# Regrouping a batched attention-times-value kernel: four heads as two half units, out stored in 8 KiB runs

## The chip, the cores and the metric

One core of one Trainium2 chip. The metric is the device time of one execution in microseconds (us), as the median of several runs. The program runs on one core. The profile's span, from the first to the last instruction, is some 1.7 to 1.8 us shorter than the timed run.

## The reference

```python
batch, n_heads, seq, head_dim = 8, 12, 1024, 64
# attn_weights: (8, 12, 1024, 1024) float32, v: (8, 12, 1024, 64) float32
out = np.einsum('bhqs,bhsd->bhqd', attn_weights, v).astype(np.float32)
```

There are 96 heads. The attention weights are 402.7 MB, v and out 25.2 MB each.

## The kernel before

Two heads at a time ("a pair", 48 of them) are loaded as 128 rows of 16 row groups, and cast from fp32 to bf16 on the way. TensorE transposes the groups (two bf16 as one fp32 word), VectorE and ScalarE copy them out to `at`, then v is multiplied with them, and the product is copied to `ot`, transposed back, copied to `osb` and stored.

```python
HELD = 9                       # stores of the last nine pairs before the last are issued after the last load
pieces_of = {                  # the last two loads come in pieces of row groups
    NP - 2: [(0, GH), (GH, GH)],
    NP - 1: [(0, 4), (4, 4), (8, 4), (12, 2), (14, 1), (15, 1)],
}

def multiply(i):
    for h in range(2):                         # head
        for half in range(2):                  # half of the row groups = half of the out partitions
            n = 0
            for kw in range(KW):
                for par in range(2):
                    last = pe.matmul(
                        out=po[h][ds(half * D, D)],            # 64 of the 128 partitions
                        lhsT=vbf[i][:, 2 * kw + par, h],       # 64 columns of v
                        rhs=at[:, ds(half * GH, GH), kw, ds(h * HP, HP), par],   # 512 columns
                        start=(n == 0), stop=(n == SB - 1),
                    )
                    n += 1
        last.then_inc(s_m[h])
# ... (cut)
def pe_direct(p):      # the last pair: each row group is multiplied as it arrives, straight into out order
    # ... (cut)
    last = pe.matmul(out=x[:, g - g0], lhsT=at[:, g, kw, :, par],
                     rhs=vbf[i][:, 2 * kw + par].rearrange("p h d -> p (h d)"), ...)
# ... (cut)
def store(p, by_sync=False):
    eng = nc.sync if by_sync else pool
    eng.wait_ge(s_out, p + 1)
    eng.dma_start(out=out_p[p].rearrange("p g d -> p (g d)"),      # 128 runs of 4 KiB
                  in_=osb[p % NO].rearrange("p g d -> p (g d)"),
                  **({} if by_sync else {"single_packet": True}))
```

## Time and profile before

| | before |
|---|---|
| time | 1056.73 us, 3 runs (1056.70 to 1056.76) |
| span of the profiled run | 1055.0 us |
| busy share of TensorE / VectorE / ScalarE | 75% / 37% / 38% |
| GpSimd's DMA queue | 99.5% of 16 engines' span |
| mean granted TensorE clock (share of full speed that the chip allowed) | 0.874 |

The prediction below shows the lines of the page, the chain and the windows. A busy share is an average over the whole run. What a change is worth is read from two stages: the beats of two pairs, which the loads set, and the tail after the last load, where the stores drain and the last pair is computed. Two more lines are needed. The first is of the timeline of before (start, length, engine, line, operation, tiles, count): the multiply of the pair before the last. The second is SyncE, which issues held stores as soon as the piece with groups 12 and 13 of the last load has landed.

```profile
1025.65 4.81 PE L173 MATMUL bank<-at,vbf 128*64 128x512 bf16 x32
...
1038.14 2.84 SPq L389 DMA_DIRECT2D out_dram<-osb  x6
```

So 32 matmuls of 512 columns take 4.81 us, 150 ns each, and at 1038.1 all of the last load had landed but its groups 14 and 15.

### The profile page before, as it was taken

The numbers are of one execution on the slowest core, as the hardware profiler recorded it, in microseconds if no ns is written. First come the engines' busy times: TensorE is split into PE (matmuls) and PEld (weight loads), VectorE is DVE, ScalarE is ACT, GpSimd is POOL, SyncE is SP. The second block draws the span as 40 slices with busy tenths as digits, with TensorE's granted clock in tenths as the row PEclk, the third lists the DMA queues.
The fourth block names the chain that finished last, engine by engine and source line by source line (L and its number), as shares of the span: only waits on it lengthen the run. The fifth ranks groups of instructions, "written<-read, shape, count | busy, mean of one in ns | idle before, by whom it ended". The sixth has DMA issues, their size and how long they took to land.

```text
span 1055.0 us, 12504 instructions
## 1 busy us (share of the span) xinstructions
PE 791.8 (75%) x5472; PEld 631.6 (60%) x5472; DVE 390.7 (37%) x585; ACT 397.6 (38%) x483; POOL 65.8 (6%) x127
## 2 busy tenths in 40 slices
PE   0897687866878678776787767877678767797797
PEld 0775476645765567555675556655566556675676
DVE  0443344333433334333343333533334333343353
ACT  0353334333434334333344333433334333353353
POOL 1010000100001000000000000000000000000020
PEclk9898878988889879898788988988879898798899
DMA  9999999999999999999999999999999999999998
GB/s 219 219 217 219 238 222 236 219 224 236 236 220 236 219 238 223 234 221 227 232 235 220 227 228 239 220 231 225 236 224 235 220 222 237 216 219 211 218 215 276
DMA packets 18590, 239.76 MB, mean 227 GB/s; under 512 B 2064, under 2 KB 2448, under 8 KB 11920
## 3 DMA queue, kind: packets, MB, share of 16 engines
q0 software_dynamic: 16992, 234.89, 99.5%
q1 hardware_dynamic: 1584, 4.72, 1.2%
q8 instruction: 4, 0.07, 0.0%
q14 instruction: 10, 0.08, 0.0%
HBM read 427.82 MB, written 25.17 MB: 429 GB/s over the span
## 4 chain that ended last, share of the span: by engine, by line
DMA 69%; PE 27%; issue 1%; POOL 1%; ACT 0%; POOLq 0%; DVE 0%; SPq 0%
DMA abf<-in_attn_weights_dram 69%; PE bank L130 23%; PE bank L145 2%; POOL vr L382 1%; PE bank L173 1%; PE bank L224 1%; ACT at L312 0%; PE bank L157 0%; ACT osb L339 0%; ACT vbf L287 0%; POOL abf L376 0%; POOLq L423 0%; DVE osb L299 0%; POOLq L476 0%; SPq L84 0%
## 5 line engine op out<-in xcount | busy, mean ns | idle before, releaser
L130 PE MATMUL bank<-ident,abf 128*128 128x128 f32 x3072 | 466.3, 324 | 256.6 <-DMA abf<-in_attn_weights_dram 256.6
L130 PEld LDWEIGHTS bank<-ident,abf 128*128 128x128 f32 x3072 | 456.4, 215 | 280.0 <-DMA abf<-in_attn_weights_dram 279.1
L312 DVE COPY at<-bank 128x1024 bf16<-128x1024 bf16 x480 | 320.6, 689 | 483.3 <-PE bank L130 481.1
L312 ACT COPY at<-bank 128x1024 bf16<-128x1024 bf16 x288 | 289.1, 1012 | 430.3 <-PE bank L130 430.3
L173 PE MATMUL bank<-at,vbf 128*64 128x512 bf16 x1504 | 226.1, 391 | 0.0
L173 PEld LDWEIGHTS bank<-at,vbf 128*64 128x64 bf16 x1504 | 111.2, 108 | 99.3 <-DVE vbf L287 7.6
L349 ACT COPY ot<-bank 128x512 f32<-128x512 f32 x47 | 27.5, 585 | 192.0 <-PE bank L173 192.0
L349 DVE COPY ot<-bank 128x512 f32<-128x512 f32 x47 | 32.5, 692 | 151.0 <-PE bank L173 151.0
L376 POOL DMA_DIRECT2D abf<-in_attn_weights_dram x54 | 28.9, 537 | 405.6 <-PE bank L130 403.0
L157 PEld LDWEIGHTS bank<-ident,ot 128*128 128x128 f32 x384 | 41.0, 140 | 20.3 <-issue 20.3
L157 PE MATMUL bank<-ident,ot 128*128 128x128 f32 x384 | 52.4, 280 | 0.0
L339 ACT COPY osb<-bank 128x512 f32<-128x512 f32 x94 | 50.5, 589 | 0.4
L145 PE MATMUL bank<-vr,spread 32*128 32x512 bf16 x384 | 50.2, 377 | 0.0
L382 POOL DMA_DIRECT2D vr<-in_v_dram x23 | 12.1, 528 | 496.4 <-PE bank L145 496.4
L287 DVE CAST vbf<-bank 128x512 bf16<-128x512 f32 x48 | 33.2, 692 | 13.6 <-PE bank L145 13.6
L287 ACT CAST vbf<-bank 128x512 bf16<-128x512 f32 x48 | 28.1, 585 | 23.3 <-PE bank L145 23.2
L145 PEld LDWEIGHTS bank<-vr,spread 32*128 32x128 bf16 x384 | 16.0, 92 | 16.4
L389 POOL DMA_DIRECT2D out_dram<-osb x41 | 22.0, 538 | 48.4 <-ACT osb L339 48.3
L224 PE MATMUL bank<-vbf,at 128*128 128x128 bf16 x128 | 8.6, 219 | 1.0 <-ACT osb L339 0.8
L224 PEld LDWEIGHTS bank<-vbf,at 128*128 128x128 bf16 x128 | 7.5, 98 | 1.7 <-ACT osb L339 1.0
L299 DVE COPY osb<-bank 64x256 f32<-64x256 f32 (+1 forms) x5 | 1.8, 361 | 6.4 <-PE bank L224 6.4
L299 ACT COPY osb<-bank 64x256 f32<-64x256 f32 (+1 forms) x5 | 1.6, 325 | 5.3 <-PE bank L224 5.3
(11 smaller groups left out, 7.1 us busy)
## 6 DMA issues: line engine op xcount, KB each, us to landing
abf<-in_attn_weights_dram POOLq DMA_DIRECT2D x46, 4096.0 KB, 32.2
out_dram<-osb POOLq DMA_DIRECT2D x41, 512.0 KB, 32.1
vr<-in_v_dram POOLq DMA_DIRECT2D x23, 512.0 KB, 12.6
abf<-in_attn_weights_dram POOLq DMA_DIRECT2D x2, 2048.0 KB, 26.6
abf<-in_attn_weights_dram POOLq DMA_DIRECT2D x3, 1024.0 KB, 19.2
out_dram<-osb SPq DMA_DIRECT2D x6, 512.0 KB, 8.3
v<-in_v_dram SPq DMA_DIRECT2D x1, 1024.0 KB, 5.2
abf<-in_attn_weights_dram POOLq DMA_DIRECT2D x1, 512.0 KB, 25.5
```

The source lines that it names most:

```text
L130: last = pe.matmul(out=pt[g % 4][:, k], lhsT=words[:, k], rhs=ident, is_transpose=True, start=(k == 0), stop=(k == KW - 1),)
L145: last = pe.matmul(out=po[h], lhsT=spread[rows, b], rhs=vr[rows, b], start=(b == 0), stop=(b == VB - 1),)
L157: last = pe.matmul(out=px[n][:, ds(j * P, P)], lhsT=ot[:, 4 * n + j].rearrange("p h q -> p (h q)"), rhs=ident, is_transpose=True, start=(j ...
L173: last = pe.matmul(out=po[h][ds(half * D, D)], lhsT=vbf[i][:, 2 * kw + par, h], rhs=at[:, ds(half * GH, GH), kw, ds(h * HP, HP), par], sta ...
L224: last = pe.matmul(out=x[:, g - g0], lhsT=at[:, g, kw, :, par], rhs=vbf[i][:, 2 * kw + par].rearrange("p h d -> p (h d)"), start=(n == 0), ...
L287: copy(out=vbf[i][:, :, h], in_=po[h].rearrange("p (k d) -> p k d", k=SB)).then_inc(s_vbf[h])
L312: ins = copy(out=at[:, g].rearrange("c k j two -> c (k j two)"), in_=bank[g % 4].bitcast(bf16),)
L339: last = nc.scalar.copy(out=halves[:, :, ds(4 * n, 4)].rearrange("p half j d -> p j half d"), in_=px[n].rearrange("p (j half d) -> p j hal ...
L349: copy(out=ot[:, :, h], in_=po[h].rearrange("p (j q) -> p j q", j=GH)).then_inc(s_ot[h])
L376: pool.dma_start(out=abf[p % 2][:, ds(g0, gn)].rearrange("p g s -> p (g s)"), in_=attn_p[p][:, ds(g0 * S, gn * S)],).then_inc(s_abf[p % 2] ...
L382: pool.dma_start(out=vr.rearrange("p b x -> p (b x)"), in_=v_g[iv]).then_inc(s_v, 16)
L389: eng.dma_start(out=out_p[p].rearrange("p g d -> p (g d)"), in_=osb[p % NO].rearrange("p g d -> p (g d)"), **({} if by_sync else {"single_ ...
```

## The change

The intent is fewer and longer runs of out. A unit is now one half of the rows of four heads; after two such units the out of four heads stands in 8 KiB runs, and is stored by one transfer. v of four heads is spread once, in the first unit. The last four heads are kept as two two-head units, and the last of them is no longer multiplied group by group. Units are numbered 0 to 47: 45 is the last four-head one, 46 and 47 are the two-head ones, and 47's load comes in four pieces. The core of the diff, with cuts:

```diff
-    HELD = 9
+    HELD = 4
     pieces_of = {
-        NP - 2: [(0, GH), (GH, GH)],
-        NP - 1: [(0, 4), (4, 4), (8, 4), (12, 2), (14, 1), (15, 1)],
+        NU - 2: [(0, GH), (GH, GH)],
+        NU - 1: [(0, 4), (4, 4), (8, 4), (12, 4)],
     }
+    attn_q = attn_weights.rearrange("b (hq four) (p r) s -> (b hq) (four p) (r s)", four=VH, p=VP)
+    out_q = out.rearrange("b (hq four) (p r) d -> (b hq) (four p) (r d)", four=VH, p=VP)
 # ... (cut)
+        def pe_unit(i, n, loaded, it):          # in the loop: 256 columns for each matmul
 # ... (cut)
+            for hp in range(2):
+                for h in range(2):
+                    for half in range(2):
+                        outs = po[hp][ds(half * D, D), ds(h * GH * VP, GH * VP)]
+                        last = multiply(outs, 2 * hp + h, half, VP, 2 * hp + h)
+                last.then_inc(s_m[hp])
+
+        def pair_half(t, half):                 # the last two units: 512 columns
+            for h in range(2):
+                last = multiply(po[h][ds(half * D, D)], 2 * t + h, half, HP, h)
+                if half == 1:
+                    last.then_inc(s_m[h])
 # ... (cut)
+        for t in range(2):
+            n = NU - 2 + t
+            for g in range(G):
+                if g in starts:
+                    pe.wait_ge(*s_piece[n, starts[g]])
+                if t == 1 and g == 12:
+                    wait_both(s_vbf, n + 1)
+                    pair_half(t, 0)
+                transpose_g(abf[t], g, n + 1)
 # ... (cut)
+            wait_both(s_last, n + 1)
+            for half in range(t, 2):
+                pair_half(t, half)
 # ... (cut)
-        def store(p, by_sync=False):
+        def store(q, by_sync=False):
 # ... (cut)
             eng.dma_start(
-                out=out_p[p].rearrange("p g d -> p (g d)"),
-                in_=osb[p % NO].rearrange("p g d -> p (g d)"),
+                out=out_q[q],
+                in_=osb[q % NO].rearrange("p r d -> p (r d)"),
```

## The prediction

> **What bounds the kernel now.** I read the page first: the 40 slices and the queues say that the transfers never rest. DMA is at 9 in every slice but the last, and the queue that GpSimd feeds is 99.5% of the span, while TensorE, the busiest compute engine, is at 75%.
>
> ```profile
> PE 791.8 (75%) x5472; PEld 631.6 (60%) x5472; DVE 390.7 (37%) x585; ACT 397.6 (38%) x483; POOL 65.8 (6%) x127
> DMA  9999999999999999999999999999999999999998
> ...
> q0 software_dynamic: 16992, 234.89, 99.5%
> ...
> HBM read 427.82 MB, written 25.17 MB: 429 GB/s over the span
> ```
>
> The HBM line is the one to keep: 453.0 MB are moved in 1055.0 us. Next, the chain that ended last, in order of time. It alternates between a wait for the attention load and 64 transposes, so each two pairs of heads form one beat, whose length is set by the loads.
>
> ```profile
> 829.35 9.69 PE bank L130 x64
> ...
> 872.95 10.03 PE bank L130 x64
> ...
> 916.54 10.37 PE bank L130 x64
> ...
> 957.65 10.31 PE bank L130 x64
> ...
> 998.75 10.28 PE bank L130 x64
> ```
>
> Columns are start, length and what. The starts are 43.60, 43.59, 41.11 and 41.10 us apart. In the first two gaps two pairs of out are stored (two loads of 8.39 MB read, one v of 1.05 MB read, two stores of 0.52 MB each); in the last two no store is issued, because the last nine pairs are held back. So two stores of 4 KiB runs cost 43.60 - 41.11 = 2.49 us of the stream, and without them it runs at (2 x 8.39 + 1.05) / 41.1 = 433.7 GB/s.
>
> Last, the stretches by window and the waits, for how far the engines are from mattering.
>
> ```profile
> 872.95:916.54 43.59, 32.99 (x224) 26.24 (x224) 16.22 (x24) 16.54 (x20) 1.58 (x3) 0.85 1.01 223
> 916.54:957.65 41.11, 33.29 (x224) 26.53 (x225) 16.12 (x24) 16.54 (x20) 1.58 (x3) 0.87 1.01 217
> ...
> 1037.00:1049.80 12.80, 12.26 (x151) 11.60 (x147) 7.06 (x13) 5.67 (x9) 0.00 (x0) 1.00 1.04 395
> 1049.80:1055.00 5.20, 0.00 (x0) 0.00 (x0) 0.00 (x0) 0.00 (x0) 0.00 (x0) 0.71 0.26 91
> ```
>
> Columns are the window, its length, busy PE, PEld, DVE, ACT, POOL, granted clock, DMA share, GB/s. PE works 33 of 41 us even in the tightest beat. In the tail (from 1037) DMA is full until about 1051 (0.26 of the last 5.2 us), draining the held stores, while PE and the copies end at 1049.8. So two things are close together there: the drain of 5.2 MB of stores, and the compute chain of the last pair.
>
> **What the Trainium skill says.** "DMA: Bandwidth & Descriptors", section "Where 436 GB/s comes from", gives 435.2 GB/s as the ceiling of the 16 ports. The trace agrees: 433.7 GB/s in the beats without stores. At that ceiling the 453.0 MB take 1040.9 us (an estimate), so no change that moves the same bytes can win 2%: the whole distance is 14 us, 1.3%, and start-up and the end take part of it. The same page, "Why small descriptors are slow (HBM only)", names a fixed cost of about three cycles for each packet. The trace's own packet records show such a term: an out packet of 4 KiB takes 159 ns, and the first v load, whose packets are 8 KiB with no change of type, 309 ns each, which is 9 ns under twice 159. "TensorE: Matmul & The Clock Gate", section "Back-to-back issue gap", has 81 ns for a weight-load-and-matmul pair of 128 columns and 131 ns for 512. Here the trace has about 61 ns (32 in 1.96 us, the last pair) and 150 ns (32 in 4.81 us, a late pair); it has none at 256. The DMA page's row "HBM row pitch at large powers of two" (section "Latency and other measured facts") reports slow copies at pitches of 2 MiB and more, and 207 GB/s per direction at 512 KiB. No run here shows it.
>
> **The change, part by part.**
>
> *Stores.* 46 pairs as 46 stores of 128 runs of 4 KiB become 23 stores of 128 runs of 8 KiB. Per store of four heads each of 16 DMA engines now has 8 packets of 309 ns for 16 of 159: 2472 for 2544 ns, 72 less, and one completion packet fewer, some 22 ns in the records. That is about 0.09 us. HELD goes from 9 pairs to 4 fours plus the last two pairs outside the scheme. Counting the issue loops, 38 pairs were stored before the last load and 19 fours are now: the same bytes. So the load stream ends 19 x 0.09 = 1.7 us earlier, and the four fours held save 0.4 us of drain.
>
> *Loads and v.* A unit is now 32 row groups of four heads: 128 runs of 64 KiB as before, at a pitch of 128 KiB instead of 64. Same packets of 32 KiB into SBUF, so the same 2432 ns each if memory does not mind the pitch. I take 0. v is queued behind the load instead of before it; it still lands some 3 us after that load, and is wanted 10 us after it. 0.
>
> *Multiplies.* 46 x 32 matmuls of 512 columns become 46 x 64 of 256. On the line through the two measured gaps (61 at 128, 150 at 512) one of 256 takes 91 ns: 64 x 91 = 5.8 us for 4.8, so a beat gains 2 us of PE. The spread of v is the same 16 matmuls per four heads, now all in the first half, where the transposes back must wait for both copies of each engine (2 x 0.69 us on DVE): perhaps 1.2 us more in that unit. PE per beat goes from 33 to some 35 or 36 us, against 41.1 without stores. The load for unit n+2 is issued after the 10.3 us of transposes of unit n, with some 10 us in hand. Nothing of it is on the path: 0.
>
> *Tail.* The last pair is no longer multiplied group by group straight into out order; it is two 64-row-partition halves, a copy to ot, a transpose back and a copy out. Its last load has one piece of four groups instead of 2, 1, 1. Working forward from the load of unit 45, 1.6 us earlier than 998.75, so 997.2: transposes 10.3, back 1.1, multiply 5.8 give 1014.4; unit 46 takes 8.0 (as the late pair of before), 2.0 for spread and back, 4.75, so 1029.2; unit 47's first twelve groups are done by 1037. Before, the gate piece (groups 12, 13) was seen at 1038.1, and the rest came 1.5 us or so later; less 1.7, the last piece is seen at about 1038.7. After it come, one behind the other, the first multiply half 2.4, four groups of transposes 2.0, their last copy 0.8, the second half 2.4, the ot copy 0.7, the transposes back 1.1 and a copy 0.6: 1048.7. The drain by then: from 1037.6, four fours of 2.47 us and one pair of 1.27 give 1048.8, so the final 512 KiB finds an almost empty queue. Issue to landing was 2.7 us at best for the 64 KB stores; 256 KiB adds some 0.7. So 1048.9 + 3.4 = 1052.3, and 2.0 from last data to end of span, as now: 1054.3 against 1055.0. The timed run is 1.7 us above the span: 1056.0. That chain is built of cautious terms, and the drain alone would allow 1054.5 or so; I put the middle at 1055.5.
>
> **The rivals.** (a) *The tail gives the gain back.* The serial chain after the last piece is about 10 us where the old one worked on groups as they came. For it: the old tail had multiplies of single groups exactly to shorten this. Against it: the old compute ended only at 1049.8 too, since PE was late and the DMA was draining anyway. It would make 1057 to 1058. (b) *TensorE becomes the bound in the beats.* If a 256-column matmul costs as much as a 512-column one (150 ns), the multiply is 9.6 us and a beat needs 43 us against 43.5 with stores and 41.1 without. This would cost up to 2 us in the last beats and delay the tail: about 1058. Against it is the 61 ns of the 128-column ones. (c) *The pitch of the loads helps or hurts.* One per cent of rate is 10 us. Against it: the loads run at the port ceiling, not at a memory limit, so there is nothing to gain and memory should have a margin. (d) *Nothing at all*: the per-packet saving is hidden by the overlap in the records (their share is 1.01), and the result is 1056.7.
>
> **Range and chances.** The expected 1.2 us gain is 0.1%. (a) and (b) push up by 1 to 2, a better tail pulls down by 1.5. I take 1053.8 to 1058.0 for 8 in 10. More than 2% faster is impossible by bytes; more than 2% slower needs (c), or a stall I did not see: 2%.
>
> **What would show it.** Beats with stores of 43.5 instead of 43.6 us, and beats without at an unchanged 41.1; out packets of 8 KiB at 309 ns; load packets still at 2432 ns; DMA at 99% or more; PE at 77 to 80% with the 256-column matmuls near 90 ns. In the tail, PE, ACT and DVE ending near 1049 and a last store of about 3.4 us. I am wrong if the beats without stores lengthen (b or c), if PE no longer waits for the attention load, or if the tail's chain ends after 1051.

## The result, and the profile after

The changed kernel takes 1059.14 us (median of 4 runs, 1058.94 to 1059.19); the kernel before took 1056.74 us beside it (1056.70 to 1057.08). The ratio is 1.0022, with a 95% interval of 1.0004 to 1.0039. It is a loss of 2.4 us where I had expected a gain of 1.2, and it lies above my range.

First the page of the changed kernel: engines, DMA slices, the queue, memory.

```profile
PE 756.6 (72%) x6856; PEld 703.3 (67%) x6856; DVE 387.6 (37%) x582; ACT 394.1 (37%) x480; POOL 54.0 (5%) x105
DMA  9999999999999999999999999999999999999997
...
q0 software_dynamic: 13824, 235.41, 99.2%
...
HBM read 427.82 MB, written 25.17 MB: 428 GB/s over the span
```

The same bytes move in fewer packets (13824 for 16992), TensorE is less busy rather than more, and the last DMA slice is thinner. Then the chain that ended last, in order of time, at the same five places as before.

```profile
828.80 9.94 PE bank L127 x64
...
872.35 10.33 PE bank L127 x64
...
915.91 9.21 PE bank L127 x64
...
957.00 9.16 PE bank L127 x64
...
998.11 10.53 PE bank L127 x64
```

The beats are 43.55, 43.56, 41.09 and 41.11 us. Those with a store are 0.04 us shorter than before, those without are unchanged. At 998.1 the changed kernel is 0.64 us ahead (998.75 before). So the loss lies after that, in the last 57 us. The end of the same chain:

```profile
1039.94 3.80 PE bank L169 x16
1043.74 2.15 PE bank L127 x16
1045.91 0.70 DVE at L286
...
1046.66 3.81 PE bank L169 x16
1050.49 0.59 ACT ot L306
...
1051.22 1.08 PE bank L154 x8
1052.33 0.69 DVE osb_last L265
```

The last piece is seen at 1039.94, and from there seven steps follow one behind the other until 1053.02. The two multiplies of 16 matmuls are the long ones, 3.8 us each. What the transfers do meanwhile is in the windows (length, busy PE, PEld, DVE, ACT, POOL, granted clock, DMA share, GB/s).

```profile
1044.00:1048.00 4.00, 3.21 (x22) 2.35 (x21) 1.98 (x3) 1.01 (x1) 0.00 (x0) 1.00 0.99 414
1048.00:1050.00 2.00, 2.00 (x10) 0.97 (x9) 0.69 (x1) 0.00 (x0) 0.00 (x0) 1.00 0.32 131
...
1051.00:1052.00 1.00, 0.78 (x7) 0.81 (x8) 0.00 (x0) 0.19 (x2) 0.00 (x0) 1.00 0.00 0
1052.00:1053.00 1.00, 0.29 (x3) 0.05 (x1) 0.68 (x1) 0.47 (x1) 0.00 (x0) 1.00 0.00 0
```

From about 1049 the stores are drained, and from 1051 to 1053 nothing moves at all: all transfers but the last two are done, and these wait for the chain. Before, the compute ended at 1049.8 while the drain went on. The bound of the tail has changed from the drain to the chain. Last, the timeline of the changed kernel shows the multiply of unit 45, with 256 columns as in the loop, that of unit 46, the counterpart of the 4.81 us line of before, and the first half multiply of unit 47 with its wait.

```profile
1009.43 4.48 PE L169 MATMUL bank<-at,vbf 128*64 128x256 bf16 x64
...
1024.04 6.55 PE L169 MATMUL bank<-at,vbf 128*64 128x512 bf16 x32
...
1039.94 3.80 PE L169 MATMUL bank<-at,vbf 128*64 128x512 bf16 x16 [1.34 <-DMA abf<-in_attn_weights_dram]
```

In unit 46 the operation, its shapes and its count are those of before, and it takes 6.55 us for 4.81: 205 ns each for 150.

### The profile page after: what moved, and what is told of

Read it like the earlier page. It is cut to its first block, busy times and chain, and to the rows that moved or that the text cites. A ratio compares the mean times of both kernels' runs of the same rounds, so it can differ in the third digit from the quotient of the medians.

```text
span 1057.4 us, 15231 instructions
## 1 busy us (share of the span) xinstructions
PE 756.6 (72%) x6856; PEld 703.3 (67%) x6856; DVE 387.6 (37%) x582; ACT 394.1 (37%) x480; POOL 54.0 (5%) x105
## 3 DMA queue, kind: packets, MB, share of 16 engines
q0 software_dynamic: 13824, 235.41, 99.2%
## 4 chain that ended last, share of the span: by engine, by line
DMA 76%; PE 22%; issue 1%; POOL 0%; DVE 0%; ACT 0%; POOLq 0%; SPq 0%
DMA abf<-in_attn_weights_dram 76%; PE bank L127 22%; PE bank L169 1%; POOL abf L328 0%; PE bank L154 0%; DVE at L286 0%; DVE osb_last L265 0%; ACT ot L306 0%; POOLq L427 0%; SPq L77 0%
## 5 line engine op out<-in xcount | busy, mean ns | idle before, releaser
L169 PE MATMUL bank<-at,vbf 128*64 128x256 bf16 (+1 forms) x3008 | 220.2, 280 | 2.1 <-DMA abf<-in_attn_weights_dram 1.3
L169 PEld LDWEIGHTS bank<-at,vbf 128*64 128x64 bf16 x3008 | 194.9, 108 | 21.8 <-DVE at L286 4.8
L154 PEld LDWEIGHTS bank<-ident,ot 128*128 128x128 f32 x392 | 43.3, 141 | 44.3 <-DVE vbf L251 42.2
L251 DVE CAST vbf<-bank 128x512 bf16<-128x512 f32 x48 | 31.0, 686 | 7.3 <-PE bank L142 7.3
L251 ACT CAST vbf<-bank 128x512 bf16<-128x512 f32 x48 | 25.9, 588 | 11.9 <-PE bank L142 11.9
L142 PE MATMUL bank<-vr,spread 32*128 32x512 bf16 x384 | 26.7, 377 | 0.0
L142 PEld LDWEIGHTS bank<-vr,spread 32*128 32x128 bf16 x384 | 10.2, 92 | 7.3
L340 POOL DMA_DIRECT2D out_dram<-osb x21 | 11.3, 540 | 41.7 <-ACT osb L265 41.7
L361 POOL TENSOR_SCALAR_AFFINE_SELECT spread<-spread 32x512 bf16<-32x512 bf16 x4 | 2.5, 628 | 0.6
```

What stands on the lines that cost most here:

```text
L142: last = pe.matmul(out=ps, lhsT=spread[rows, b], rhs=vr[rows, b], start=(b == 0), stop=(b == VB - 1),)
L154: last = pe.matmul(out=px[k][:, ds(j * P, P)], lhsT=ot[:, 4 * k + j], rhs=ident, is_transpose=True, start=(j == 0), stop=(j == 3),)
L169: last = pe.matmul(out=outs, lhsT=vbf[:, 2 * kw + par, h], rhs=at[:, ds(half * GH, GH), kw, ds(col * np_, np_), par], start=(n == 0), stop ...
L251: copy(out=vbf[:, :, h], in_=ps.rearrange("p (k d) -> p k d", k=SB)).then_inc(s_vbf[e])
L340: eng.dma_start(out=out_q[q], in_=osb[q % NO].rearrange("p r d -> p (r d)"), **({} if by_sync else {"single_packet": True}),).then_inc(s_e ...
L361: pool.affine_select(out=spread[ds(h * VP, VP)], in_=spread[ds(h * VP, VP)], compare_op=mybir.AluOpType.not_equal, fill=1.0, base=0, patte ...
```

## The experiments

**Theory A**: matmuls to different halves of the out partitions overlap where the program switches from one half to the other. `pair_half` has the half outside and the head inside, so 16 matmuls in a row go to the same 64 partitions, and the half multiplies of unit 47 have no switch at all. This makes the serial chain after the last piece long, and that chain sets the end. **Rival B**: TensorE is late in the tail as a whole. **Rival C**: the drain of the stores sets the end, as before. **Rival D**: a matmul costs the same in any order, and only the number of matmuls after the last piece counts. The experiments ran in three batches on three chips, each with the kernel before beside them (medians of 1056.84 to 1056.97 us); the changed kernel was not run again in them, so 1059.14 stands for it throughout.

### Order of unit 46's multiply alone

```diff
+        def pair_whole(t):
+            for h in range(2):
+                for half in range(2):
+                    last = multiply(po[h][ds(half * D, D)], 2 * t + h, half, HP, h)
+                last.then_inc(s_m[h])
 # ... (cut)
-            for half in range(t, 2):
-                pair_half(t, half)
+            if t == 0:
+                pair_whole(t)
+            else:
+                pair_half(t, 1)
```

> Only unit 46's multiply is put back into the order of before (head outside, half inside). Theory A (switching between the two halves of the output partitions lets matmuls overlap; the last unit's chain sets the end): its 32 matmuls take 4.8 us instead of 6.55, TensorE then waits about 3 us instead of 1.3 for the last piece, and the time stays at 1059.1 (within 0.3), because unit 46 is hidden behind that piece. Rival B (TensorE runs late into the tail and every microsecond counts): 1057.4. Rival C (the drain of the stores sets the end): 1059.1 too.

Measured: 1060.34 us (4 runs, 1059.11 to 1061.49). The multiply did come back to 4.81 us. The time did not stay, though: it rose by 1.2 us and spread over 2.4 us. The chain of the profiled run (1061.49 us) shows where, and the windows why.

```profile
1040.90 5.13 PE bank L169 x16
```

```profile
1038.00:1040.00 2.00, 0.21 (x2) 0.02 (x1) 0.46 (x1) 1.26 (x2) 0.00 (x0) 1.00 1.02 397
1040.00:1042.00 2.00, 1.10 (x3) 0.52 (x4) 0.00 (x0) 0.00 (x0) 0.00 (x0) 0.59 0.99 410
1042.00:1044.00 2.00, 2.00 (x6) 0.79 (x5) 0.00 (x0) 0.00 (x0) 0.00 (x0) 0.56 1.04 438
```

TensorE, now early, waits 2.69 us for the last piece instead of 1.34. The granted clock falls to 0.59 and 0.56, and the half multiply then takes 5.13 us instead of 3.80. In the changed kernel the clock stayed at 1.00 over its shorter wait. (In this run the piece also came 1.0 us later, because two beats of the stream were longer, 43.78 and 44.10 us; such beats turn up in several runs.) So in this profiled run getting early to the wait cost 1.3 us in the chain; the fastest of the four runs, 1059.11 us, was no slower than the changed kernel. Rival B, which wanted 1057.4, is refuted.

### First half multiply of unit 47 ahead of the wait

```diff
+                if t == 1 and g == 12:
+                    for x in range(2):
+                        pe.wait_ge(s_cp[6 + x], n + 1)
+                    wait_both(s_vbf, n + 1)
+                    pair_half(t, 0)
                 if g in starts:
                     pe.wait_ge(*s_piece[n, starts[g]])
-                if t == 1 and g == 12:
-                    wait_both(s_vbf, n + 1)
-                    pair_half(t, 0)
```

> Only the first half multiply of unit 47 is moved ahead of the wait for the last piece. Theory A: it starts at 1038.6 when group 11 is transposed, ends at 1042.4, so the groups 12 to 15 start 1.3 us earlier than 1043.7: 1057.8. Rival C (drain of the stores): no change, 1059.1.

Measured: 1057.98 us (1057.85 to 1058.30), as Theory A had it (1057.8). In its chain the half multiply starts at 1038.70 and the groups 12 to 15 at 1042.43, 1.3 us earlier than 1043.74. Rival C would have left 1059.1.

### Both

The two edits above together.

> Both of the edits before. Theory A: TensorE reaches the half multiply about 1.8 us earlier and ends it at 1040.7, just after the piece lands at 1039.9, so the chain is 3.0 us shorter: 1056.1. The two parts are then not additive (0 and 1.3 alone, 3.0 together). Rival C: 1059.1.

Measured: 1056.82 us (1056.69 to 1057.06); Theory A wanted 1056.1. The half multiply runs 1037.7 to 1041.4, 0.7 us later than expected, because TensorE had to wait for the piece with groups 8 to 11, seen at 1035.52; and the chain's copies end at 1050.69 instead of 1053.02, 2.3 us earlier, so the parts are not additive: +1.2 and -1.2 alone, -2.3 together. The order of unit 46 is worth something only where the time is filled with work; the clock then stayed at 1.00 until the copies. The kernel before took 1056.88 us in these rounds, so these two edits alone bring the change back to level.

### All of unit 47 after the last piece, but with switches

```diff
-                if t == 1 and g == 12:
-                    wait_both(s_vbf, n + 1)
-                    pair_half(t, 0)
 # ... (cut)
-            if t == 0:
-                wait_both(s_vbf, n + 1)
+            wait_both(s_vbf, n + 1)
             wait_both(s_last, n + 1)
-            for half in range(t, 2):
-                pair_half(t, half)
+            if t == 0:
+                for half in range(2):
+                    pair_half(t, half)
+            else:
+                pair_whole(t)
```

> Unit 47 multiplies everything after the last piece, 32 matmuls with the halves alternating each 8, instead of 16 before and 16 after groups 12 to 15, both after the piece. The same 32 matmuls stand after the piece. Theory A (alternation matters): 4.8 us in place of 3.8 + 3.8, so 2.8 us less: 1056.3. Rival D (a matmul costs the same in any order, the count after the piece is what matters): 1059.1.

Measured: 1057.00 us (1056.69 to 1057.37). The same 32 matmuls stand after the same wait, and still 2.1 us are gained. In its chain they are one entry:

```profile
1043.20 4.80 PE bank L169 x32
```

4.80 us in place of 3.80 + 3.81. This refutes Rival D most plainly. (`pair_whole` is that of the first experiment. Theory A wanted 1056.3; the copies end at 1050.54, 2.5 us earlier and not 2.8.)

### Halves alternating from matmul to matmul

Units 46 and 47 multiply at their end as above, with the loop over `half` moved innermost.

```diff
+            for h in range(2):
+                n = 0
+                for kw in range(KW):
+                    for par in range(2):
+                        for half in range(2):
+                            last = pe.matmul(
+                                out=po[h][ds(half * D, D)],
 # ... (cut: operands as before, start=(n == 0), stop=(n == SB - 1))
+                        n += 1
+                last.then_inc(s_m[h])
```

> Units 46 and 47 multiply at once at their end, with the halves alternating from one matmul to the next. Theory A: one matmul each 113 ns, 32 in 3.7 us (6.55, and 3.8 + 3.8, now), so the chain from the last piece is 3.9 us shorter; the drain of the stores then comes close and takes part of it: 1055.3 to 1055.8. If alternating that finely does no more than each 8: 4.8 us, 1056.3. Rival D: 1059.1.

Measured: 1057.75 us (1056.26 to 1058.49), which misses 1055.3 to 1055.8. The matmuls did as expected, on the timeline:

```profile
1040.62 3.65 PE L127 MATMUL bank<-ident,abf 128*128 128x128 f32 x16 [2.69 <-DMA abf<-in_attn_weights_dram]
1045.25 3.83 PE L214 MATMUL bank<-at,vbf 128*64 128x512 bf16 x32 [0.99 <-DVE at L297]
```

32 of them in 3.83 us, 120 ns each, where the two half multiplies of unit 47 took 3.80 and 3.81. Of the 3.8 us won there, 1.5 were lost in the line above it: after a wait of 2.69 us the 16 transposes take 3.65 us where they took 2.20 in the changed kernel, and the windows give a clock of 0.67 and 0.50 from 1040 to 1044. Another 0.7 went because the piece came later (1040.62 for 1039.94). The copies end at 1051.64, 1.4 us earlier than 1053.02, and the time is 1.4 us lower.

### The kernel before, with the halves outside

```diff
-            for h in range(2):
-                for half in range(2):
+            for half in range(2):
+                for h in range(2):
 # ... (cut)
-                last.then_inc(s_m[h])
+                    if half == 1:
+                        last.then_inc(s_m[h])
```

> The kernel before with only the order of its multiply changed: half outside, head inside, as the changed kernel has it in its last two units. Theory A: each multiply of 32 takes 6.55 us instead of 4.81, hidden in the beats (they stay at 43.6 and 41.1 us), but in the tail the pairs 45 and 46 run back to back without waiting, so the last copies end 3.5 us later than 1049.8 and the time is 1059.5 to 1060.2. Rival D (the order is free): 1056.7.

Measured: 1058.47 us (1057.37 to 1058.82); before 1056.84. Two lines of its timeline, the multiply of the pair before the last and VectorE's last copy:

```profile
1027.32 6.55 PE L173 MATMUL bank<-at,vbf 128*64 128x512 bf16 x32
```

```profile
1052.91 0.28 DVE L300 COPY osb<-bank 64x128 f32<-64x128 f32 x1 [0.53 <-PE bank L225]
```

The order alone turns 4.81 into 6.55 us in the other kernel too, and the beats stay (median 43.58). The copies end at 1053.2, 3.4 us later than 1049.8, just as expected, but the time grew by only 1.6 us: I had expected 2.8 or more. The kernel before has slack between its compute and its end.

### The kernel before, with the halves alternating

The same edit as in the alternating run, in `multiply` of the kernel before.

> The kernel before with the halves alternating from one matmul to the next in its multiply. Theory A: 32 matmuls in 3.8 us instead of 4.81 in every pair; in the tail the last copies end some 2 us earlier than 1049.8. The time of the kernel before is set by the drain of its stores (transfers busy to the end), so it stays at 1056.7 or gains at most 0.5. If its compute chain set the end: 1054.7.

Measured: 1056.88 us (1056.64 to 1056.96), before 1056.97. The multiply took 3.81 us, and VectorE's last copy is

```profile
1047.75 0.28 DVE L299 COPY osb<-bank 64x128 f32<-64x128 f32 x1 [0.53 <-PE bank L224]
```

```profile
1048.00:1050.00 2.00, 0.00 (x0) 0.00 (x0) 0.03 (x1) 0.01 (x1) 0.00 (x0) 1.00 1.01 407
```

The copies end 1.8 us earlier than before, and in the two microseconds after them the transfers still run at a share of 1.01. There is no gain: the tail of the kernel before is set by the drain, that of the changed kernel by the chain.

### The store of four heads as two transfers of 4 KiB runs

```diff
-            eng.dma_start(
-                out=out_q[q],
-                in_=osb[q % NO].rearrange("p r d -> p (r d)"),
# ... (cut)
+            src = osb[q % NO].rearrange("p r d -> p (r d)")
+            for k in range(2):
+                cols = ds(k * G * D, G * D)
+                eng.dma_start(
+                    out=out_q[q][:, cols],
+                    in_=src[:, cols],
# ... (cut)
```

(The waits for their semaphores count 32 instead of 16.)

> The changed kernel with each store of four heads issued as two transfers of 4 KiB runs; all else equal. It takes away the 8 KiB runs alone. If these saved 0.04 us for each four heads (beats 43.57 against 43.61): the beats go to 43.61, the load stream ends 0.75 us later, and the time is 1059.9. If the 0.09 us of my prediction were right, 1060.8. If the shorter beat comes from elsewhere (order of v, of issues): 1059.1.

Measured: 1061.53 us (5 runs, 1060.09 to 1061.82), more than any theory wanted. Some beats of its chain:

```profile
393.90 10.44 PE bank L127 x64
...
437.49 9.28 PE bank L127 x64
...
481.09 9.66 PE bank L127 x64
```

43.59 and 43.60 us, which is also the median of its beats with stores (43.60), where the changed kernel has 43.56 and the kernel before 43.59. The edit brings back two transfers for each four heads as well as the shorter runs, so the two together are worth 0.04 us for each four heads, 0.8 us over 19 of them, which gives 1059.9; the fastest run, 1060.09, is near that. The other 1.6 us of the median (1.4 in the profiled run) I can only partly place: in the profiled run four of the beats with stores took 43.75 to 44.13 us (two in the changed kernel's run were longer than 43.6, 43.75 at most), and the load of unit 45 was seen at 1000.25, 2.1 us later. Why the stream has more of such beats with split stores stays open.

### Five fours held instead of four

```diff
-    HELD = 4
+    HELD = 5
```

> Five fours held back until after the last load instead of four. Theory A (the end is the chain from the last piece, with the transfers idle some 3 us before the last two stores): the loads end 2.47 us earlier, the chain with them: 1056.7. Rival C (drain of the stores sets the end, so holding more gains nothing): 1059.1 or more.

Measured: 1056.99 us (1056.56 to 1057.11). The load of unit 45 is seen at 995.83 instead of 998.11, and the chain's copies end at 1050.72 instead of 1053.02, both 2.3 us earlier. One more store could be moved behind the last load for nothing, because the transfers had been idle there. This is against Rival C.

### All mends together

The two edits of order and place, with HELD = 5 and, in another run, 6.

> The mended order of unit 46, the first half multiply of unit 47 ahead of the last wait, and five fours held back. Theory A with the drain as its floor: the chain ends 2.4 us earlier than in the kernel with the first two edits alone, so near 1048.3; the held stores keep the transfers busy to about 1050.5, then the last two stores: 1054.6 to 1055.2, faster than both kernels by some 2 us. If the drain were already the bound in the kernel with two edits (1056.8), no gain.

Measured: 1056.46 us (5 runs, 1055.76 to 1057.37). The copies end at 1048.58, close to the 1048.3 expected, and 2.1 us earlier than with the two edits alone, yet the time falls by only 0.4 us and misses 1054.6 to 1055.2.

> As the run before with six fours held. The chain ends another 2.4 us earlier, but the same bytes have to drain, so if the drain is the floor by now: within 0.3 us of the run before. If the chain still counts: 2 us faster still.

Measured: 1055.77 us (4 runs, 1055.52 to 1056.77), before 1056.97; ratio 0.9991, interval 0.9975 to 1.0006. The copies end at 1045.43, another 3.2 us earlier, and the time moves by 0.7 us, within the spread of the two: nearer the forecast for the drain (0.3) than that for the chain (2). The window after the copies is now full of transfers:

```profile
1044.00:1048.00 4.00, 0.70 (x7) 0.46 (x5) 0.69 (x1) 0.59 (x1) 0.00 (x0) 0.84 1.00 418
```

So the drain is most likely the bound again. This is the fastest version measured, 1.2 us below the kernel before in the medians, though the interval still holds 1.

## Why the prediction was wrong

The bound, the size of what could be won and the beats were read rightly; the tail was mis-sized. Term by term:

- **Stores.** Predicted 0.09 us for each four heads. The packet records agree with the sum (8 KiB packets at 309 ns, 4 KiB at 159), but only 0.03 to 0.04 us of it reaches the beat (medians of 43.59 before, 43.56 in the change, 43.60 in the split-store run). So the load of unit 45 came 0.64 us earlier, not 1.6.
- **Loads and v.** Predicted 0, and right: beats without stores stayed at 41.1 us and load packets at 2432 ns, so the larger pitch cost nothing.
- **Multiplies in the beats.** I took 91 ns for 256 columns; 64 took 4.48 us, 70 ns each. TensorE's share fell to 72% where I wrote 77 to 80%. My Rival (b) was wrong. The wait for the spread copies was 1.3 us per four heads (predicted 1.2). None of it mattered, as predicted.
- **Last piece.** "The rest came 1.5 us or so later; less 1.7, the last piece is seen at about 1038.7." As it stands this sum gives 1037.9, so a slip of 0.8 us is in it, too. The piece was seen at 1039.94. The rest is two groups of 16, one eighth of a load: 2.4 us at 433.7 GB/s. With 0.64 for the 1.7 this gives 1038.14 + 2.4 - 0.64 = 1039.9. This is 1.2 us of the error: 0.9 for the rest of the load and 1.1 for the stream, less the slip.
- **The step that failed most**: "the first multiply half 2.4 ... the second half 2.4". I took 16 times the 150 ns of a late pair, without seeing that those 150 ns come from switching halves every eight matmuls, which `pair_half` doesn't do. They took 3.8 and 3.8 us: 2.8 us of the error. The runs with the order changed, in both kernels and in both directions, show this: 233 to 238 ns each with no switch, 205 with one switch in 32 matmuls, 150 with three, 120 with one after every matmul. The rest of the chain was 0.3 us longer than my sum.
- **Last store.** Predicted 5.6 us from the last copy to the end of the span, measured 4.4 (1053.02 to 1057.4): 1.2 us in the other direction.

Together 1.2 + 2.8 + 0.3 - 1.2 = 3.1 us, which is the way from the 1056.0 of my sum to 1059.1. That the slip of 0.8 and the last store took 2.0 us off the error is luck. The drain came as I had it (done at 1048.8 predicted, about 1049 seen), and one of my own signs of being wrong came true: the tail's chain ended after 1051, at 1053.0. I then moved the sum to 1055.5, calling its terms cautious; they were not. My Rival (a), that the tail gives the gain back, was right in kind, and I set it at 1057 to 1058. The counter-argument I gave it, that the old compute ended late too, was true and beside the point: the old tail could be late because its drain was longer than its compute, as the alternating run of the kernel before shows (1.8 us earlier, no gain).

One reading of the prediction is weaker than it sounds, though nothing above hangs on it. The 433.7 GB/s that I set beside the ceiling of the ports counts the fp32 bytes read from memory; after the cast the windows show 217 GB/s moved. So the trace does not show that the ports limit the loads. At 433.7 GB/s the 453.0 MB take 1044.5 us (an estimate), with the same conclusion.

The overlap itself, as far as seen: in the trace's start times of single matmuls in the pair of before, most starts are some 225 ns apart, but around each of the three switches four pairs start within 6 to 33 ns of one another; unit 46 after has one switch, and four pairs within 5 to 34 ns around it. It also changes its bank twice without changing the half, after 8 and after 24 matmuls, and no pair is seen there: so it is the half that counts, not the bank. Which two matmuls make up a pair the records do not tell. The Trainium skill, "TensorE: Matmul & The Clock Gate", section "Part 3: Packing small matmuls — row/col tiling", describes that matmuls placed in different 32-wide tiles of the array run concurrently, with some 4 ns between their starts. The trace agrees with the concurrency for halves of 64 columns; the starts here are 5 to 34 ns apart. I had read the gap section of that page, and not this one.

The lower clock after a longer wait is of the kind that the same page describes in "Part 1: The HAM clock gate (the "warmup" mystery)": an idle stretch brings TensorE to half rate, with a window of about 3.4 us that runs freely. Here 2.69 us of waiting sufficed in two profiled runs, and 1.34 us did not. The other waits bear this out: in the thirteen kept traces, from 60 us on, none of TensorE's 235 idle stretches of 1 to 1.86 us is followed by a fall to half clock within 3 us, and 561 of the 562 of 1.98 us or more are. What ran before and after the waits was not varied.

## What to carry to other kernels

Before taking a matmul's time from another place in the trace, compare the order of the output partitions around it (with 64-column weights the same matmul cost 120 to 238 ns here). In a tail, write down both clocks, the drain of the transfers and the serial chain from the last piece of data, for the kernel before and after; a change that lengthens the one with slack costs nothing, until it becomes the longer one. And fill a wait before the last burst with work that can be done early, because the wait may lower TensorE's clock.

## What the Trainium skill lacked or had wrong

- "TensorE: Matmul & The Clock Gate", Part 3, says that matmuls keep program order in start and end. After runs of eight matmuls in one column half, a strict order would let one pair overlap at a switch; four pairs of starts within 6 to 33 ns are seen at each. That the order is not strict here is inferred from this count, as the records do not name the matmul.
- The same page, "Back-to-back issue gap", gives 131 ns for a matmul of 512 columns in a stream of weight loads and matmuls, and some 216 ns for an isolated one, without naming the order of the output partitions. Here 120 to 238 ns were seen for 512 columns with 64-column weights, by order alone, and 70 ns for 256 columns with a switch every eight.
- The same page, Part 1, ties the fall to the low clock to an idle window of about 3.4 us. A wait of 2.69 us was followed by a clock of 0.59 and 0.56 here, and waits from 1.98 us on were followed by half clock within 3 us (561 of 562).
- The same page, Part 4, says that the high clock does not engage for transposes. In the kernel before, a burst of 64 transposes alone began at a clock of 0.50 (480.4 to 484.0) and ended at 1.00 (487.0 to 490.4).
- No page tells what longer out runs are worth under a full queue: 0.03 to 0.04 us for each 1 MiB, going from two transfers of 4 KiB runs to one of 8 KiB runs.
